# Latent attention rows: transpose and division by the row sum in one matmul with a scaled identity

## The chip, the cores and the metric

The kernel runs on one core of a Trainium2 chip. The metric is the device time of one execution in microseconds (us). The kernel before takes 1691.37 us, the median of three runs that lie between 1691.06 and 1694.24.

The core has five engines that run side by side, each taking its own instructions in order, and that wait for one another by semaphores. PE is the matrix engine: a matmul is a weight load (LDWEIGHTS, listed as PEld) followed by a MATMUL that streams the other operand through the array, and it writes into PSUM. DVE (the vector engine) and ACT (the scalar engine) do elementwise work and move results from PSUM to SBUF. POOL does a few small things, and SP issues most of the DMAs.

## The reference

Two layers of a hybrid backbone over 512 latent tokens with a prefix of 256 context tokens, width 1024, float32. Layer 0 mixes by a gated linear attention and, beside it, by a grouped attention of 8 query heads on 2 key heads of width 64; layer 1 is a gated recurrence. Each layer ends with a SwiGLU feed-forward of width 2816. The part that matters here is the attention of layer 0 for the latent rows, in which each query sees all 768 keys:

```
def _softmax_attend(q, k, v):
    s = jnp.einsum('bhgqd,bhkd->bhgqk', q, k, preferred_element_type=jnp.float32) * (ATT_HEAD_DIM ** -0.5)
    p = jax.nn.softmax(s, axis=-1).astype(v.dtype)
    return jnp.einsum('bhgqk,bhkd->bhgqd', p, v)
```

The softmax is exp(s - max) divided by the sum of its row. The second einsum sums over keys, so the kernel has to turn the probabilities: from queries on partitions to keys on partitions.

## The kernel before, in words

Tokens are handled in tiles of P = 128: LT = 4 latent tiles, NTT = 6 tiles in all, NT = 768 tokens. The attention of layer 0 is the class `Attention`. Its method `latent` (a generator, called "y" in the list of steps that sets the program's order) goes through 32 steps, 4 query tiles by 8 heads. A step i does the following, where `ahead` is 3:

- `scores` for head i: four matmuls write the 128 x 768 scores into a PSUM tile `S` (two buffers of 1024 columns). DVE takes the row extreme into `amx` (L193), ACT takes the exponential into the SBUF tile `prob` and sums each row into `asm` on the way (L195), DVE takes the reciprocal into `ars` (L196), and DVE multiplies the 768 columns of `prob` by it in place (L198).
- `turned` for head i - 3: six transposes on PE, each of a 128 x 128 block of `prob` with the identity `ident` as the other operand. The first four write one PSUM bank (tag "tr", two buffers), the last two write a bank that they share with the attention's output of the other parity (`sc0` or `sc1`). ACT copies the bank with 512 columns to `probT`; the one with 256 columns is copied by ACT, or by DVE for every fourth head (`j % 4 == 3`).
- `values` for each second head: `attO` sums the products of `probT` with the values over six key tiles, for two heads at once in the two halves of the array's columns.
- after the fourth pair of a query tile, `done` splits the output into a high and a low part (L734 on ACT, L735 on DVE) for the output projection.

Between these steps the program places others: transposes and splits of the linear attention's output (`catT`, L1288, L1289), its normalization (`gvo`), the turning of the next query tile's queries (`qT`, `qs`), a group of modulation columns (`mod_acc`), and weight splits for the next stage (`wH`, `wL`).

In this stretch all PE instructions are pinned to the order in which the code emits them; DVE and ACT are ordered by the framework's scheduler, so an edit may move their instructions. All PE instructions are issued by two helpers, so matmuls carry the line L355 (`Net.mm`) and transposes L358 (`Net.tr`), and it is the tile's name that tells them apart.

One later place of the kernel already multiplies by a scaled identity: `pair_turn` in the norm ahead of layer 1's mixer. L689 makes a tile `dg` from the identity and the inverse root mean square, and the turning of two token tiles is done in four rounds of four matmuls with it:

```
        for q in range(4):
            pt = self.tr_tile(f"hT{t}{q}").rearrange("p (k i) -> p k i", k=2)
            ...
            for kk in range(2):
                k = 2 * q + kk
                for a, (xt, dg) in enumerate(pair):
                    self.mm(pt[:, kk, a * P : (a + 1) * P], xt[:, k * P : (k + 1) * P], dg, start=True, stop=True)
```

It runs for three pairs of token tiles, so it holds 3 x 4 x 4 = 48 matmuls in the code, all of them of float32 operands with 128 columns.

Of the kernel before, what the change touches and what calls it, by code (L numbers as in the profile page):

```python
# [8 lines left out]
F32 = mybir.dt.float32  # L9
# [4 lines left out]
ALU = mybir.AluOpType  # L14
# [3 lines left out]
P = 128  # L18
# [115 lines left out]
class Attention:  # L134
# [40 lines left out]
            nc.vector.tensor_tensor(q[half[1 - n], 4 * n : 4 * n + 4, :], pv[half[n]], H.bitcast(F32), op=ALU.subtract)  # L175
        self.q[t] = q

    def scores(self, t, heads, p):

        nc, net = self.nc, self.net  # L180
        s = net.mm_tile("S")
        nk = p.shape[-1]
        w = 1024 // len(heads)
        for x, hd in enumerate(heads):
            at = w * x
            for ks in self.k[int(t >= LT)]:
                m = ks[0].shape[-1]
                for i, k in enumerate(ks):
                    net.mm(s[:, at : at + m], self.q[t][:, hd, :], k[:, hd // 4, :], start=(i == 0), stop=(i == 1))
                at += m  # L190
        sv = s.rearrange("p (x k) -> p x k", k=w)[:, :, :nk]
        mx, sm, r = (net.sm.tile([P, len(heads)], F32, tag=tag, name=tag) for tag in (("amx", "asm", "ars") if len(heads) == 1 else ("ms4", "ss4", "rs4")))
        nc.vector.tensor_reduce(mx, sv, axis=AX.X, op=ALU.min)  # L193
        for x in range(len(heads)):
            nc.scalar.activation(p[:, x, :], sv[:, x, :], AF.Exp, bias=mx[:, x : x + 1], scale=-1.0, accum_out=sm[:, x : x + 1])  # L195
        nc.vector.reciprocal(r, sm)  # L196
        for x in range(len(heads)):
            nc.vector.tensor_scalar(p[:, x, :], p[:, x, :], r[:, x : x + 1], None, op0=ALU.mult)  # L198

    def turned(self, p, pT, vector, which=None):  # L200

        nc, net = self.nc, self.net
        n = pT.shape[1]
        for b, g in enumerate(range(0, n, 4)):
            m = min(4, n - g)
            pt = net.tr_tile("pT") if b == 0 or which is None else net.sc_tile("pT", which)
            for i in range(m):
                net.tr(pt[:, i * P : (i + 1) * P], p[:, (g + i) * P : (g + i + 1) * P], net.ident)
            src = pt[:, : m * P].rearrange("p (c i) -> p c i", c=m)
            (nc.vector.tensor_copy if b in vector else nc.scalar.copy)(pT[:, g : g + m, :], src)  # L210

# [23 lines left out]
    def context(self):  # L235
# [24 lines left out]
        yield  # L260
        queries(LT + 1, "wL")
        scores(0)
        yield
        scores(1)
        yield
        turned(0)
        yield
        scores(2)
        values(0)
        yield  # L270
        scores(3)
        turned(1)
        yield
        values(1)
        yield
        self.done(LT)
        turned(2)
        yield
        values(2)
# [5 lines left out]
    def latent(self, ap):  # L285
        kl = [ap.tile([P, 2, SEQ], F32R, name=f"k{x}") for x in "HL"]
        self.k[0] = [kl] + self.k[1]
        q = lambda t: ap.tile([P, 8, P], F32R, tag="qs", bufs=2, name=f"qs{t}")
        self.keys(0, LT, kl)
        yield  # L290
        self.queries(0, q(0))
        yield

        ahead = 3
        ps, pTs, due = {}, {}, []
        for i in range(8 * LT + ahead + 2):
            t, hd = divmod(i, 8)
            if t < LT:
                ps[i] = ap.tile([P, NT], F32, tag="prob", bufs=4, name="prob")
                self.scores(t, (hd,), ps[i][:, None, :])  # L300
            j = i - ahead
            if 0 <= j < 8 * LT:
                pTs[j] = ap.tile([P, NTT, P], F32, tag="probT", bufs=4, name="probT")
                self.turned(ps.pop(j), pTs[j], (1,) if j % 4 == 3 else (), self.other())
            if due:
                t0, n, xs = due.pop()
                self.values(t0, n, xs)
                if n == 3:
                    self.done(t0)
            if 0 <= j < 8 * LT and j % 2:  # L310
                due.append((j // 8, j // 2 % 4, [pTs.pop(x) for x in (j - 1, j)]))
            if t + 1 < LT and hd == 4:
                self.queries(t + 1, q(t + 1))
            yield
# [1883 lines left out]
```

## Time and profile before

| | |
|---|---|
| time, median of three runs | 1691.37 us |
| time of the profiled execution | 1690.72 us |
| its span, first to last instruction | 1688.8 us |
| PE busy in the span | 1646.5 us (97%) |
| DVE busy | 1309.0 us (78%) |
| ACT busy | 922.0 us (55%) |
| the latent heads' turning, first to last transpose | 264.1 to 344.9 us |
| granted clock of PE, mean | 0.998 |

A row of a tile's view gives, for a group of like instructions, the line, engine, operation, output and inputs, the count, and the shortest, median and longest duration in ns. A row of the timeline gives the start and the length in us of a run of like instructions, and in brackets the time that the engine stood idle before them and what it waited for. A row of the waits says who waited for what, the sum in us, the count, and the longest. The table by stretches gives each engine's busy time and, in brackets, its instructions. Matmuls overlap each other in PE's pipeline: the sum of their durations is larger than the time that they take, and their price is read from the distance between their starts.

### The profile page before, as it was taken

How to read it: one execution, taken by the hardware profiler on the slowest of the kernel's cores; microseconds unless marked ns; L12 is line 12 of the kernel's file. 1: busy time of each engine (PE TensorE's matmuls, PEld its weight loads, DVE VectorE, ACT ScalarE, POOL GpSimd, SP SyncE). 2: the span in 40 equal slices, each digit the busy share in tenths (PEclk: the TensorE clock that was granted, in tenths of full speed). 3: DMA queues.
4: the chain of work that ended last, by engine and by line, in shares of the span. 5: the costliest groups of instructions: out<-in, count | busy, mean ns of one | idle time of the engine just before them, and what ended most of it. 6: DMA issues, size and time to landing. Idle time of an engine off the chain costs nothing.

```text
span 1688.8 us, 32537 instructions
## 1 busy us (share of the span) xinstructions
PE 1646.5 (97%) x13407; PEld 1482.6 (88%) x13407; DVE 1309.0 (78%) x2102; ACT 922.0 (55%) x1563; POOL 124.4 (7%) x129
## 2 busy tenths in 40 slices
PE   6999998999999999999999999999999999999997
PEld 5899997888999999998887888888888899999875
DVE  4889768875898988778667538788774599987977
ACT  4745567836544443445447436566564565555654
POOL 1004110011000000003102000000000100000221
PEclk9999999999999999999999999999999999999999
DMA  9651003164243444348625542121124334333793
GB/s 329 192 155 41 2 27 101 51 211 153 86 138 103 147 150 139 115 146 180 125 101 186 172 128 64 51 62 41 52 65 149 125 113 117 108 101 101 192 195 137
DMA packets 184737, 204.79 MB, mean 121 GB/s; under 512 B 7143, under 2 KB 141837, under 8 KB 184589
## 3 DMA queue, kind: packets, MB, share of 16 engines
q1 hardware_dynamic: 173632, 181.82, 34.3%
q0 software_dynamic: 9024, 17.30, 6.0%
q10 hardware_dynamic: 1932, 3.59, 0.6%
q8 instruction: 105, 1.72, 0.4%
q14 instruction: 44, 0.35, 0.1%
HBM read 193.23 MB, written 9.46 MB: 120 GB/s over the span
## 4 chain that ended last, share of the span: by engine, by line
PE 84%; DVE 7%; ACT 4%; DMA 2%; issue 2%; POOL 1%; DVEq 0%; ACTq 0%; POOLq 0%
PE nat L355 12%; PE a L355 12%; PE ff L355 8%; PE E L355 8%; PE x L355 7%; PE oproj L355 6%; PE o L355 4%; PE D L355 4%; PE b L355 4%; PE fq L355 3%; PE gqk L355 2%; PE pearly L355 2%; PE S L355 1%; PE poh L355 1%; PE attO L355 1%
## 5 line engine op out<-in xcount | busy, mean ns | idle before, releaser
L355 PE MATMUL nat<-wH,x 128*128 128x256 f32 (+2 forms) x968 | 225.4, 321 | 3.0 <-ACT x L734 2.6
L355 PEld LDWEIGHTS nat<-wH,x 128*128 128x128 f32 x968 | 162.2, 190 | 19.2 <-ACT x L734 3.6
L824 ACT CAST wH<-raw 128x1024 fp32r<-128x1024 f32 x120 | 125.0, 1050 | 95.5 <-DVE raw L849 31.8
L825 DVE TENSOR_TENSOR wL<-raw,wH 128x1024 fp32r<-128x1024 f32 x120 | 145.7, 1221 | 20.8 <-ACT wH L824 20.2
L355 PE MATMUL nat<-wL,x 128*128 128x256 f32 (+2 forms) x484 | 153.4, 317 | 0.3 <-DVE wL L770 0.3
L770 DVE TENSOR_TENSOR wL<-raw,wH 128x1024 fp32r<-128x1024 f32 (+1 forms) x83 | 98.7, 1198 | 46.1 <-ACT wH L769 45.4
L355 PE MATMUL ff<-x,wH 128*128 128x512 f32 (+1 forms) x512 | 127.6, 340 | 0.0
L668 POOL TENSOR_TENSOR rs<-ms,neghalf 128x1 f32<-128x1 f32 (+2 forms) x62 | 66.4, 1076 | 785.4 <-DVE ms L666 785.3
L769 ACT CAST wH<-raw 128x1024 fp32r<-128x1024 f32 (+1 forms) x83 | 84.9, 1035 | 69.5 <-PE ff L355 19.8
L355 PE MATMUL oproj<-wH,x 128*128 128x512 f32 x320 | 102.0, 395 | 0.4 <-ACT x L1288 0.4
L597 DVE SCALAR_TENSOR_TENSOR macc<-mraw,scT,macc 128x1024 f32<-128x1024 f32 x70 | 88.2, 1281 | 14.7 <-DMA mraw<-in_mod_w_dram 14.7
L355 PEld LDWEIGHTS nat<-wL,x 128*128 128x128 f32 x484 | 92.1, 190 | 6.0 <-DVE wL L770 0.7
L355 PEld LDWEIGHTS ff<-x,wH 128*128 128x128 f32 x512 | 87.3, 190 | 10.0
L355 PE MATMUL x<-wH,two 128*128 128x512 f32 x280 | 91.4, 396 | 0.9 <-DVE y L1796 0.7
L976 ACT COPY qkh<-arr 128x512 f32<-128x512 f32 x112 | 70.1, 642 | 36.3 <-DVE arr L981 32.2
L1721 POOL DMA_DIRECT2D t<-in_ffn_w_down_dram x36 | 41.8, 1229 | 648.2 <-DVE wL L1755 610.4
L355 PE MATMUL ff<-x,wL 128*128 128x256 f32 (+1 forms) x256 | 86.2, 337 | 0.0
L849 DVE TENSOR_TENSOR raw<-raw 128x512 f32<-128x512 f32 x120 | 82.8, 690 | 2.8
L981 DVE TENSOR_TENSOR arr<-arr,f 128x512 f32<-128x512 f32 x112 | 74.2, 687 | 1.9 <-ACT qkh L976 0.3
L355 PE MATMUL E<-x,wH 128*128 128x384 f32 (+1 forms) x320 | 70.9, 311 | 0.0
L355 PE MATMUL b<-x,wH 128*128 128x384 f32 (+1 forms) x320 | 70.6, 309 | 0.0
L355 PE MATMUL a<-T,wH 128*128 128x384 f32 (+1 forms) x320 | 70.4, 309 | 0.1
(422 smaller groups left out, 4536.8 us busy)
## 6 DMA issues: line engine op xcount, KB each, us to landing
mraw<-in_mod_w_dram SPq DMA_DIRECT2D x80, 512.0 KB, 4.6
raw<-in_ffn_w_gate_dram SPq DMA_DIRECT2D x44, 512.0 KB, 4.8
raw<-in_ffn_w_up_dram SPq DMA_DIRECT2D x44, 512.0 KB, 4.3
raw<-in_odd_w_in_dram SPq DMA_DIRECT2D x40, 512.0 KB, 3.7
t<-in_ffn_w_down_dram POOLq DMA_DIRECT2D x30, 512.0 KB, 8.0
raw<-in_ffn_w_down_dram SPq DMA_DIRECT2D x28, 512.0 KB, 7.3
mraw<-in_mod_w_dram SPq DMA_DIRECT2D x32, 256.0 KB, 6.0
raw<-in_even_w_in_dram SPq DMA_DIRECT2D x16, 512.0 KB, 4.2
```

Of the source, the lines that this page charges most:

```text
L355: return self.pin(self.nc.tensor.matmul(*a, **k))
L597: nc.vector.scalar_tensor_tensor(a, u, w, a, op0=ALU.mult, op1=ALU.add)
L668: nc.gpsimd.tensor_tensor(rs, ms, self.neghalf.to_broadcast([P, w]), op=ALU.pow)
L769: nc.scalar.copy(H[:, :m], raw[:, :m])
L770: nc.vector.tensor_tensor(L[:, :m], raw[:, :m], H[:, :m].bitcast(F32), op=ALU.subtract)
L824: self.nc.scalar.copy(H, f)
L825: self.nc.vector.tensor_tensor(L, f, H.bitcast(F32), op=ALU.subtract)
L849: add = lambda o, x, y: nc.vector.tensor_tensor(o, x, y, op=ALU.add)
L976: nc.scalar.copy(qkv[:, :, :, half, :], dst)
L981: nc.vector.tensor_tensor(dst, dst, tb, op=ALU.mult)
L1721: add = lambda o, src: self.pin(nc.gpsimd.dma_start(out=o, in_=src, accum_op=ALU.add))
```

## The change

For the latent rows the probabilities are no longer multiplied by the inverse sums. Instead DVE makes a 128 x 128 tile `dg`, the identity with its rows scaled by the inverse sums, and the six transposes of a head become six ordinary float32 matmuls of the `prob` block with `dg`: the result is the block turned, with each column scaled. There are four buffers of `dg`. Beside it, the 256-column bank is copied by DVE for every second head instead of every fourth. The context rows go on as before.

```diff
-    def scores(self, t, heads, p):
+    def scores(self, t, heads, p, dg=None):
...
         nc.vector.reciprocal(r, sm)
+        if dg is not None:
+            nc.vector.tensor_scalar(dg, net.ident, r, None, op0=ALU.mult)
+            return
         for x in range(len(heads)):
             nc.vector.tensor_scalar(p[:, x, :], p[:, x, :], r[:, x : x + 1], None, op0=ALU.mult)
...
             for i in range(m):
-                net.tr(pt[:, i * P : (i + 1) * P], p[:, (g + i) * P : (g + i + 1) * P], net.ident)
+                at, x = pt[:, i * P : (i + 1) * P], p[:, (g + i) * P : (g + i + 1) * P]
+                if dg is None:
+                    net.tr(at, x, net.ident)
+                else:
+                    net.mm(at, x, dg, start=True, stop=True)
...
-                self.scores(t, (hd,), ps[i][:, None, :])
+                dgs[i] = ap.tile([P, P], F32, tag="dg", bufs=4, name="dg")
+                self.scores(t, (hd,), ps[i][:, None, :], dgs[i])
...
-                self.turned(ps.pop(j), pTs[j], (1,) if j % 4 == 3 else (), self.other())
+                self.turned(ps.pop(j), pTs[j], (1,) if j % 2 else (), self.other(), dgs.pop(j))
```

On PE the order stays, and in the code's own count so does the number of instructions: one for one. This is what stands on PE at the third head of the first query tile (`kH`, `kL` and `kc` are the keys, high and low parts of the latent ones and those of the context, `qs` the queries), before:

```order
L358 MATMUL pT<-ident,prob 128x128 x6
L355 MATMUL attO<-probT,natk 64x128 x12
L355 MATMUL S<-kH,qs_3589 128x512
L355 MATMUL S<-kL,qs_3589 128x512
L355 MATMUL S<-kc,qs_3589 128x256 x2
```

and after (the helpers' lines have moved by eight, L355 to L363 and L358 to L366):

```order
L363 MATMUL pT<-dg,prob 128x128 x6
L363 MATMUL attO<-probT,natk 64x128 x12
L363 MATMUL S<-kH,qs_3589 128x512
L363 MATMUL S<-kL,qs_3589 128x512
L363 MATMUL S<-kc,qs_3589 128x256 x2
```

The six `pT` are now issued by the helper for matmuls; nothing has changed place. On ACT the scheduler has moved some instructions. At the start of the stage, behind the first two exponentials and the split of the context rows' output, there stood before:

```order
L734 CAST x_3653<-attO 128x4x128
L210 COPY probT<-pT 128x512
L195 ACTIVATE prob,asm<-S,amx 128x768 x2
L210 COPY probT<-pT 128x256
L210 COPY probT<-pT 128x512
L210 COPY probT<-pT 128x256
L195 ACTIVATE prob,asm<-S,amx 128x768
```

and after:

```order
L742 CAST x_3653<-attO 128x4x128
L195 ACTIVATE prob,asm<-S,amx 128x768
L217 COPY probT<-pT 128x512
L195 ACTIVATE prob,asm<-S,amx 128x768
L217 COPY probT<-pT 128x256
L217 COPY probT<-pT 128x512
L195 ACTIVATE prob,asm<-S,amx 128x768
```

The third exponential now stands ahead of the first copy, and one of the 256-column copies has gone to DVE. On DVE the copies stand between the row extremes of two heads; around the end of the first query tile (`x` here is L735, the split of that tile's output), before:

```order
L193 TENSOR_REDUCE amx<-S 128x1
L196 RECIPROCAL ars<-asm 128x1
L198 TENSOR_SCALAR prob<-prob,ars 128x768
L196 RECIPROCAL ars<-asm 128x1
L198 TENSOR_SCALAR prob<-prob,ars 128x768
L193 TENSOR_REDUCE amx<-S 128x1
L735 TENSOR_TENSOR x_3654<-attO,x_3653 128x4x128
```

and after:

```order
L193 TENSOR_REDUCE amx<-S 128x1
L196 RECIPROCAL ars<-asm 128x1
L198 TENSOR_SCALAR dg<-ident,ars 128x128
L196 RECIPROCAL ars<-asm 128x1
L198 TENSOR_SCALAR dg<-ident,ars 128x128
L743 TENSOR_TENSOR x_3654<-attO,x_3653 128x4x128
L193 TENSOR_REDUCE amx<-S 128x1
L217 COPY probT<-pT 128x256
```

Here the split of the output stands ahead of the row extreme that it stood behind, and the scaling works on 128 columns instead of 768. POOL's and SP's instructions are the same in both kernels.

More of the change, by code (lines that the diff above doesn't have):

```diff
@@ L196, in scores, with turned @@
         nc.vector.reciprocal(r, sm)
+        if dg is not None:
+            nc.vector.tensor_scalar(dg, net.ident, r, None, op0=ALU.mult)
+            return
         for x in range(len(heads)):
             nc.vector.tensor_scalar(p[:, x, :], p[:, x, :], r[:, x : x + 1], None, op0=ALU.mult)
-    def turned(self, p, pT, vector, which=None):
+    def turned(self, p, pT, vector, which=None, dg=None):
         nc, net = self.nc, self.net
@@ L294, in latent @@
         ahead = 3
-        ps, pTs, due = {}, {}, []
+        ps, pTs, dgs, due = {}, {}, {}, []
         for i in range(8 * LT + ahead + 2):
```

## The prediction, made before the changed kernel ran

> **What bounds the kernel now.** I read first the page's busy times, then a table by stretches around the place of the change, then PE's waits in that stretch.
>
> ```profile
> span 1688.8 us, 32537 instructions
> PE 1646.5 (97%) x13407; PEld 1482.6 (88%) x13407; DVE 1309.0 (78%) x2102; ACT 922.0 (55%) x1563; POOL 124.4 (7%) x129
> ```
>
> PE is nearly always busy over the whole run. That is an average, so the stage is looked at by itself: the turning of the latent heads lies between 264.1 and 344.9 us.
>
> ```profile
> 254.00:262.00 8.00, 5.20 (x49) 4.24 (x50) 6.72 (x11) 7.64 (x10) 0.61 (x1) 1.00 0.81 255
> 262.00:348.00 86.00, 81.16 (x819) 68.08 (x816) 70.44 (x131) 67.23 (x142) 1.28 (x1) 1.00 0.20 69
> 348.00:1689.00 1341.00, 1322.55 (x9321) 1195.00 (x9319) 1038.10 (x1538) 704.57 (x1115) 83.47 (x81) 1.00 0.43 123
> ```
>
> The columns are the stretch, its length, and busy time with instruction count of PE, PEld, DVE, ACT and POOL, then granted clock, DMA share, GB/s. In the 86.0 us from 262 on, PE is busy 81.16, DVE 70.44, ACT 67.23, at full clock. PE stands still for 4.8 us, and the waits on PE in this stretch account for all of it:
>
> ```profile
> PE pT L358 <- DVE x L735: 1.8, 2, 1.3
> PE S L355 <- ACT prob L195: 1.8, 2, 1.4
> PE pT L358 <- DVE probT L210: 0.5, 2, 0.3
> PE qT L358 <- ACT probT L210: 0.5, 1, 0.5
> PE catT L358 <- DVE qs L175: 0.2, 1, 0.2
> ```
>
> 1.8 + 1.8 + 0.5 + 0.5 + 0.2 = 4.8 us. So here PE sets the pace, and whatever DVE or ACT save can be worth 4.8 us at most, while work added to PE has no more than 4.8 us of idle time to go into. None of these waits is on L198, the scaling that the change removes.
>
> **The six products of a head on PE.** The diff puts one matmul for one transpose, so the question is what each holds PE for. The rows by tile, of the turning and of the later place that already multiplies by a scaled identity of the same type and size:
>
> ```profile
> L358 PE MATMUL pT<-ident,prob x224: 270/272/330, 234.7 to 344.9; 128*128 128x128 f32 x112
> L355 PE MATMUL hT<-dg,xr x96: 270/275/377, 906.9 to 946.7; 128*128 128x128 f32 x96
> ```
>
> Two things are to be seen. The durations, 272 and 275 ns, are alike and say nothing of the price, since PE overlaps its instructions. The counts do: the code has 48 matmuls with `dg` at the later place (three pairs, four rounds, four each) and the trace has 96, so a float32 matmul is run as two weight loads and two MATMULs. Of the transposes the code has 192 in the latent rows and 32 in the context rows, and the trace has 224: one each. What one record takes is read from the timeline, from a run of each kind:
>
> ```profile
> 277.08 0.82 PE L358 MATMUL pT<-ident,prob 128*128 128x128 f32 x6
> 277.65 0.47 PE L355 MATMUL S<-kH,qs 128*128 128x512 f32 x1
> ...
> 906.90 1.05 PE L355 MATMUL hT<-dg,xr 128*128 128x128 f32 x8
> 907.70 0.48 PE L355 MATMUL x<-wH,aH 128*128 128x512 f32 x1
> ```
>
> Six transposes span 0.82 us; less the last one's own 0.272, five distances make 0.548, or 0.110 us each. Eight records with `dg` span 1.05; less 0.275, seven distances make 0.775, or 0.111 us each. The pace of a record is the same, only there are two per matmul. A head goes from 6 x 0.110 = 0.66 us to 12 x 0.111 = 1.33 us, 0.67 more, and 32 heads give **+21.5 us** of PE. This is my firmest term; from the same two runs, timed from the start to the start of the next tile, it is 6 x 0.095 = 0.57 against 12 x 0.100 = 1.20, or +20.2 us, which I take as its low end. The high end is 32 x (12 x 0.112 - 6 x 0.108) = +22.3, from the rounding of the rows.
>
> The Trainium skill's page "TensorE: Matmul & The Clock Gate", Part 4, gives a PE transpose as about 275 ns in one kernel's context and says that the fast clock does not engage for it. By that price a transpose would be dearer than the two records, and 192 x (0.222 - 0.275) = -10 us. The trace agrees with the 275 as a duration (272 here), and disagrees with it as a price: the transposes start 0.110 us apart, and the granted clock of the stretch is 1.00.
>
> **DVE.** The rows of what goes and of the nearest thing to what comes:
>
> ```profile
> L198 DVE TENSOR_SCALAR prob<-prob,ars x32: 600/620/624, 261.7 to 341.4; 128x768 f32<-128x768 f32 x32
> L689 DVE TENSOR_SCALAR dg<-ident,rs x6: 281/285/287, 896.5 to 934.7; 128x128 f32<-128x128 f32 x6
> L210 DVE COPY probT<-pT 128x256 f32<-128x256 f32 x8 | 3.3, 414 | 3.2 <-PE pT L358 3.2
> L210 ACT COPY probT<-pT 128x256 f32<-128x256 f32 x24 | 9.2, 382 | 0.5 <-PE pT L358 0.3
> ```
>
> 32 x (0.620 - 0.285) = 10.7 us less, and eight copies more (32 of 256 columns in all, 16 instead of 8 on DVE), 8 x 0.414 = 3.3: DVE loses 7.4 us of its 70.4. **ACT** loses 8 x 0.382 = 3.1 of its 67.2. Both I cost at nothing by themselves: PE is busy beside them, and they can only shorten PE's 4.8 us of waits. The way from the sum of a row to the first product is shorter by 0.335 us for each head; three heads of lead hide that already, as no wait of `pT` on `ars` or L198 shows. A `dg` buffer is used again by the fourth head after it, whose scores PE makes only behind the products that read it, so no wait comes from there.
>
> **What becomes of PE's 4.8 us.** PE now arrives later at each wait, by up to 0.67 us a head, unless what it waits for follows from PE itself. The four largest:
>
> ```profile
> 266.39 0.47 PE L355 MATMUL S<-kH,qs 128*128 128x512 f32 x1 [1.44 <-ACT prob L195]
> 288.59 0.41 PE L358 MATMUL pT<-ident,prob 128*128 128x128 f32 x2 [1.30 <-DVE x L735]
> 312.70 0.66 PE L358 MATMUL qT<-ident,natq 128*128 128x128 f32 x4 [0.51 <-ACT probT L210]
> 332.01 0.44 PE L358 MATMUL pT<-ident,prob 128*128 128x128 f32 x2 [0.50 <-DVE x L735]
> ```
>
> The first is the backlog of exponentials on ACT at the stage's start. One head's turning lies ahead of it (0.67), and the third exponential now stands ahead of a 512-column copy, whose median is 577 ns by this row:
>
> ```profile
> L210 ACT COPY probT<-pT x60: 371/577/613, 235.3 to 345.1; 128x512 f32<-128x512 f32 x36, 128x256 f32<-128x256 f32 x24
> ```
>
> Together 1.25, so about 0.2 of 1.44 stays. The waits on L735 follow from PE: the bank is that of the attention's output, which ends on PE a few matmuls earlier and must pass ACT and DVE. Between that end and the waiting product PE has four products of the first bank, 4 x (0.222 - 0.110) = 0.45 us more work, so 1.30 becomes 0.85 and 0.50 becomes 0.05. The order of DVE puts L735 ahead of a row extreme there, which may take away more, and I leave that out. The remaining waits, 4.8 - 1.44 - 1.80 = 1.6 us, I take as gone, as PE is late by several heads' worth and DVE and ACT have less to do. That leaves 0.2 + 0.85 + 0.05 = 1.1 us, so 3.7 us of the added work falls into idle time.
>
> A new wait could come from DVE's copies, 16 instead of 8, each behind whatever DVE is doing. Two of the eight of before held PE, for 0.5 us together. Eight more at that rate give 0.5, at 0.3 each 2.4. With 0.67 us more between two uses of the bank I take nothing.
>
> **After the stage.** The output projection and the feed-forward follow at once:
>
> ```profile
> 347.00:380.00 33.00, 33.00 (x155) 27.29 (x152) 25.46 (x27) 10.75 (x15) 4.43 (x4) 1.00 0.68 222
> sum 193.00, PE 193.00 PEld 178.31 DVE 153.51 ACT 94.96 POOL 11.30; mean PE 38.60 PEld 35.66 DVE 30.70 ACT 18.99 POOL 2.26
> ```
>
> From 347 to 540 us PE is busy 193.0 of 193.0, so what the stage loses is handed on whole. Farther on there is 1341.00 - 1322.55 = 18.5 us in which PE is not busy; a lead that DVE and the DMAs win while PE is late can give little back there, as it would have to last through 190 us without a gap.
>
> **The sum.** +21.5 - 3.7 = +17.8 us on the profiled execution's 1690.72 gives 1708.5. The median of the runs stands 0.65 above that execution, so 1691.37 + 17.8 = 1709.2: I say **1709**. Its own range is 1705 (20.2 of PE, all 4.8 absorbed, another 1.5 given back later) to 1713 (22.3 of PE, 1 absorbed).
>
> **The rivals.**
>
> - *Faster: ACT and DVE set the pace, and PE has room.* It speaks for it that the chain of work that ended last passes through DVE and ACT repeatedly in this stage, L198 among them (start, length, piece):
>
> ```profile
> 270.95 0.62 DVE prob L198
> ...
> 304.55 0.59 DVE prob L198
> ```
>
> If all the added products fitted into idle time and all five waits went, it would be 1691.4 - 4.8 = 1686.6. It decides from the point at which PE has 21 us of idle time in the stage, and it has 4.8. Chance 0.03.
> - *The matmul with `dg` is one record, as the transpose.* Then the change does what its words say, division for nothing, and DVE's 7.4 us can only shorten waits: 1687 to 1691, middle 1689. Against it stand 96 records for 48 matmuls. Chance 0.03.
> - *Transposes hold PE for their listed duration.* -10 us, 1681; the pace of 0.110 us speaks against it, chance 0.01. This is the skill's price above.
> - *No cushion.* The waits stay, and DVE's copies add theirs: 21.5 + 2.4 = +23.9, 1715. For it: waits that hang on PE's own work move along with it. Against it: DVE and ACT each have less to do. From 1713 up, chance 0.12.
> - *More given back.* DVE's and the DMAs' lead shortens later waits: 1700 to 1705. Against it: no gap for 190 us. Chance 0.07.
>
> **How the numbers follow.** The forecast has 0.74 (1705 to 1713). To leave out no more than 2 in 10 I take in most of the no-cushion and half of the given-back case: 1703 to 1715. No change means within 0.2%, 3.4 us, which is about what a measurement of this kernel can tell. Faster by more than that: 0.03 + 0.01 and a third of the one-record case, 0.05; the same: 0.02; slower: 0.93.
>
> **What the profile after would show.** `pT` with `dg` counted 384 times, in runs of twelve at 0.111 us, and only 32 transposes left under the old form; if there are 192, the main term is wrong. The scaling at 285 ns instead of 620, and DVE's busy time in the stage some 7 us lower. PE's waits in the stage near 1 us instead of 4.8, the wait of `S` on the exponential nearly gone, a rest on L735's successor. PE busy without a gap behind the stage, each landmark there some 18 us later. A wait of `pT` on DVE's copies above 1 us would speak for no cushion.

## The result: 15 us slower

The changed kernel takes 1706.92 us (median of four runs, 1706.46 to 1708.3) against 1691.64 for the kernel before on the same chip, a ratio of 1.0088 with a 95% interval from 1.0076 to 1.0099, so 12.9 to 16.8 us. Timed again it was 1705.49 against 1691.71, ratio 1.0078 (1.0066 to 1.0091). The profiled execution took 1706.46, 15.7 more than the one of before.

The page after, and the stretch in which the latent heads are turned, now 102 us long instead of 86 (columns as before):

```profile
span 1704.7 us, 32915 instructions
PE 1666.8 (98%) x13599; PEld 1507.0 (88%) x13599; DVE 1303.2 (76%) x2110; ACT 921.8 (54%) x1555; POOL 124.0 (7%) x129
```

```profile
262.00:364.00 102.00, 101.49 (x1005) 91.65 (x1006) 65.77 (x141) 65.98 (x134) 1.00 (x1) 0.98 0.18 60
```

PE has 192 instructions more (13599 against 13407) and is now busy for 101.49 of 102 us. DVE was busy for 70.4 us in the 86 before and for 65.8 in the 102 after, and the run is slower all the same.

The products and the making of `dg`, in the view by tile:

```profile
L363 PE MATMUL pT<-dg,prob x384: 272/275/421, 266.1 to 361.9; 128*128 128x128 f32 x192
L366 PE MATMUL pT<-ident,prob x32: 270/272/328, 235.4 to 259.3; 128*128 128x128 f32 x32
L198 DVE TENSOR_SCALAR dg<-ident,ars x32: 274/286/290, 262.5 to 356.5; 128x128 f32<-128x128 f32 x32
```

Two records per product, 384 for 192, and the median duration of one hardly differs from that of a transpose. What a head costs PE is seen in the timeline, first of the kernel after, then of the kernel before, each with a run that is followed by the next scores and one that is followed by the output's products:

```profile
280.67 1.50 PE L363 MATMUL pT<-dg,prob 128*128 128x128 f32 x12
281.93 0.47 PE L363 MATMUL S<-kH,qs 128*128 128x512 f32 x1
...
282.70 1.50 PE L363 MATMUL pT<-dg,prob 128*128 128x128 f32 x12
284.13 1.53 PE L363 MATMUL attO<-probT,natk 128*64 128x128 f32 x24
```

```profile
274.06 0.82 PE L358 MATMUL pT<-ident,prob 128*128 128x128 f32 x6
274.81 1.53 PE L355 MATMUL attO<-probT,natk 128*64 128x128 f32 x24
```

From start to start it is 1.26 and 1.43 us after. Before it was 0.57 (the pair at 277.08 and 277.65 that the prediction shows) and 0.75. That is 0.68 to 0.69 us a head, or 21.9 us for 32 heads. The waits on PE in the stage, after:

```profile
PE attO L363 <- ACT probT L217: 2.1, 1, 2.1
PE pT L366 <- DVE kL L162: 0.6, 1, 0.6
PE pT L363 <- DVE probT L217: 0.2, 1, 0.2
```

The first two lie ahead of the first latent product and were there before (2.1 and 0.6). Of the 4.8 us behind it, 0.2 is left.

How the 15.7 us of the profiled pair come about: the stage, from the first latent scores to the last products of the output, takes 16.2 us more. The first pair of rows is of before, the second of after:

```profile
255.83 0.47 PE L355 MATMUL S<-kH,qs 128*128 128x512 f32 x1
...
345.95 1.52 PE L355 MATMUL attO<-probT,natk 128*64 128x128 f32 x22
```

```profile
256.56 0.48 PE L363 MATMUL S<-kH,qs 128*128 128x512 f32 x1
...
362.89 1.52 PE L363 MATMUL attO<-probT,natk 128*64 128x128 f32 x22
```

That is 106.33 - 90.12 = 16.2. It is +21.9 for the products; -5.7 for stalls that are gone; +1.2 because in this execution PE ran for 3.4 us at half clock just there, so that the eight scores matmuls ahead of the first product took 2.72 us (263.36 to 266.08) instead of 1.50; and -0.8 because three matmuls of the output projection, which stood among the last heads' transposes, are now behind them. (The description of the change says that PE's order stays. This is the exception to it.) These terms sum to 16.6, 0.4 more than measured. Behind the stage the 0.8 comes back, and the execution of before had its own stretch at half clock at 902 us, which the one after has not: about 1.7 us. So 16.2 + 0.7 of later start + 0.8 - 1.7 = 16.0, against 15.9 between the spans. That the two stretches at half clock nearly cancel in this pair is chance.

The stalls need a word, since they are larger than the list of waits says. In the kernel before I took, for each run of six transposes, the distance from its start to the start of the next tile, less the shortest such distance with the same neighbour. Ten runs are longer, by 1.69, 1.49, 0.72, 0.67, 0.57, 0.50, 0.49, 0.43, 0.06 and 0.06 us: 6.7 us in all, where the list has 4.8. After, four runs are longer, by 1.0 together, and 0.36 of that is no wait but the first run's share of the half-clock stretch. Two examples from the timeline of before:

```profile
286.69 0.60 PE L358 MATMUL pT<-ident,prob 128*128 128x128 f32 x4
288.59 0.41 PE L358 MATMUL pT<-ident,prob 128*128 128x128 f32 x2 [1.30 <-DVE x L735]
288.84 0.60 PE L358 MATMUL qT<-ident,natq 128*128 128x128 f32 x4
...
306.01 0.82 PE L358 MATMUL pT<-ident,prob 128*128 128x128 f32 x6
307.15 0.50 PE L355 MATMUL S<-kH,qs 128*128 128x512 f32 x1 [0.32 <-ACT prob L195]
```

The first run takes 288.84 - 286.69 = 2.15 us where an unstalled one takes 0.66, a stall of 1.49 that is listed as 1.30. The second takes 1.14 instead of 0.57, a stall of 0.57 that is listed as 0.32. The duration of the last record before a wait still counts as busy while nothing new can start.

### The profile page after: what moved, and what is told of

Its sections match the earlier page's. It is cut to its first block, busy times and chain, and to the rows that moved or that the text cites. A ratio compares the mean times of both kernels' runs of the same rounds, so it can differ in the third digit from the quotient of the medians.

```text
span 1704.7 us, 32915 instructions
## 1 busy us (share of the span) xinstructions
PE 1666.8 (98%) x13599; PEld 1507.0 (88%) x13599; DVE 1303.2 (76%) x2110; ACT 921.8 (54%) x1555; POOL 124.0 (7%) x129
## 4 chain that ended last, share of the span: by engine, by line
PE 86%; DVE 6%; ACT 3%; DMA 2%; issue 2%; POOL 1%; ACTq 0%; POOLq 0%; DVEq 0%
PE nat L363 11%; PE a L363 11%; PE ff L363 8%; PE E L363 7%; PE x L363 7%; PE oproj L363 5%; PE o L363 5%; PE b L363 4%; PE D L363 4%; PE fq L363 3%; PE pT L363 2%; PE gqk L363 2%; PE pearly L363 2%; PE S L363 2%; PE q L363 2%
## 5 line engine op out<-in xcount | busy, mean ns | idle before, releaser
L363 PE MATMUL nat<-wH,x 128*128 128x256 f32 (+2 forms) x968 | 225.4, 321 | 3.0 <-ACT x L742 2.6
L363 PEld LDWEIGHTS nat<-wH,x 128*128 128x128 f32 x968 | 162.2, 190 | 19.2 <-ACT x L742 3.7
L363 PE MATMUL nat<-wL,x 128*128 128x256 f32 (+2 forms) x484 | 153.4, 317 | 0.3 <-DVE wL L778 0.3
L363 PE MATMUL ff<-x,wH 128*128 128x512 f32 (+1 forms) x512 | 127.6, 340 | 0.0
L363 PE MATMUL oproj<-wH,x 128*128 128x512 f32 x320 | 101.9, 395 | 0.6 <-ACT x L1296 0.6
L363 PEld LDWEIGHTS nat<-wL,x 128*128 128x128 f32 x484 | 92.1, 190 | 6.0 <-DVE wL L778 0.8
L363 PEld LDWEIGHTS ff<-x,wH 128*128 128x128 f32 x512 | 87.3, 190 | 10.0
L363 PE MATMUL x<-wH,two 128*128 128x512 f32 x280 | 90.5, 392 | 0.9 <-DVE y L1804 0.7
L363 PE MATMUL ff<-x,wL 128*128 128x256 f32 (+1 forms) x256 | 86.2, 337 | 0.0
L363 PE MATMUL E<-x,wH 128*128 128x384 f32 (+1 forms) x320 | 70.9, 311 | 0.0
L363 PEld LDWEIGHTS oproj<-wH,x 128*128 128x128 f32 x320 | 59.5, 188 | 12.8 <-ACT x L1296 1.1
L363 PE MATMUL a<-x,dH 128*128 128x384 f32 (+1 forms) x320 | 70.3, 309 | 0.3 <-ACT early L905 0.3
```

The lines of the kernel that those rows point to most:

```text
L363: return self.pin(self.nc.tensor.matmul(*a, **k))
```

## The experiments

Theory A was that the loss is the 192 second records, less the stalls that PE's added work fills by itself. The main rivals were that the savings on DVE and ACT soften the loss (B), that a float32 product is dearer in itself (D), and that the copies on DVE matter (F).

**The products alone.** The kernel before, with this edit in `turned` for the latent rows:

```diff
-                net.tr(at, x, net.ident)
+                net.mm(at, x, net.ident, start=True, stop=True)
```

> Only the products: the latent rows' transposes become float32 matmuls with the plain identity, while DVE's scaling of 768 columns and the copies stay as before. Theory A (PE sets the pace; 192 more records cost 21.9 us of PE, less the time that PE stood still before, which it fills by itself): 14 to 17 us slower than before, 1706 to 1709, about as the changed kernel. Theory B (what softened the loss from 21.5 to 15.3 us is the 7.4 us that DVE and the 3.1 us that ACT saved): without these savings the waits stay, 19 to 22 us slower, 1711 to 1714.

Measured: 1704.72 us against 1691.23, ratio 1.0086 (1.0072 to 1.0100), 13.5 us slower. No saving on DVE or ACT, and yet it is not slower than the changed kernel. Its waits on PE in the stage:

```profile
PE attO L359 <- ACT probT L214: 2.1, 1, 2.1
PE pT L362 <- DVE kL L162: 0.6, 1, 0.6
PE S L359 <- ACT prob L195: 0.4, 1, 0.4
```

The waits are gone just as well with the large scaling still on DVE. So what took them away is PE's own slowness, not the work spared elsewhere. B falls. The loss is half a microsecond less than A's lowest; the first measurement of the changed kernel stood 2.2 us above it, which is followed up below.

**Everything but the products.** The changed kernel, with plain transposes in place of the products (so it leaves out the division by the row sums):

```diff
-                    net.mm(at, x, dg, start=True, stop=True)
+                    net.tr(at, x, net.ident)
```

> Everything but the products: the small scaled identity is made and the scaling of 768 columns is gone, the copies are divided as in the changed kernel, but the blocks are turned by plain transposes (the scaled identity is not used, so the division by the sums is left out). PE's work is that of before, so only waits on PE can go. Theory A1 (the time that PE stands still in the stage is about 7 us, counted from start to start of its instructions): 4 to 7 us faster, 1684.5 to 1687.5. Theory A2 (it is the 4.8 us of the list of waits): 2 to 4.8 us faster, not below 1686.8. Theory C (DVE and ACT have nothing to do with the pace): within 1.5 us of before.

Measured: 1691.28 us against 1691.23, ratio 1.0002 (0.9993 to 1.0011). That can't be told from none. I had expected 2 to 7 us, since DVE has less to do:

```profile
262.00:348.00 86.00, 81.47 (x821) 68.36 (x819) 63.32 (x139) 65.29 (x134) 1.01 (x1) 1.00 0.20 69
```

DVE is busy for 63.3 us instead of 70.4, and PE for as long as before. The waits on PE in it, without the two ahead of the stage:

```profile
PE pT L363 <- DVE x L740: 1.5, 2, 1.3
PE S L360 <- ACT prob L195: 1.4, 1, 1.4
PE pT L363 <- DVE probT L214: 1.2, 4, 0.5
PE qT L363 <- DVE x L1294: 0.2, 1, 0.2
```

4.3 us of 4.8 are still there. The two largest single waits, 1.3 and 1.4 us, hang on a chain that starts on PE (the output's last products, ACT's cast, DVE's subtraction, then the bank is free) and on ACT's exponential. The waits for copies even went from 0.5 to 1.2. Both A1 and A2, which I held, fall, and C's range holds: the part of the change that was to gain is, as a whole, worth nothing here.

**The copies alone.** The kernel before with `(1,) if j % 2 else ()` instead of `(1,) if j % 4 == 3 else ()`.

> The kernel before with one edit: DVE instead of ACT copies the 256-column bank for every second head, not every fourth. The vector part as a whole measured no difference (1691.3 against 1691.2). Theory F (it is the sum of two: the smaller scaling gains, the copies on DVE lose about as much): 2 to 5 us slower than before, 1693 to 1696. Theory C (neither matters, since PE waits for work that hangs on PE itself): within 1.5 us of before.

Measured: a ratio of 1.0005 (0.9996 to 1.0013), 1693.14 against 1691.51 in the medians. The interval ends at 2.2 us, at the low edge of F, so the times do not decide between F and C. The trace leans to F. PE's waits for copies on DVE are 2.1 us in the stage, where there were 0.5:

```profile
PE pT L358 <- DVE probT L210: 2.1, 5, 0.8
```

From start to start this kernel's stalls are 9.1 us where the kernel before has 6.7. A half-clock stretch makes 0.4 of that, so about 2 us are new. The kernel with everything but the products has the same copies and the small scaling, and its stalls are 6.7 us again. So in these traces, of one execution each, the vector part is a loss of about 2 us by the copies and a gain of about 2 us by the smaller scaling. In the times neither is clear of the noise, and the smaller scaling with the old copies was not run.

**The transposes twice.** The kernel before, each latent transpose issued two times into the same place:

```diff
-                net.tr(at, x, net.ident)
+                for _ in range(2):
+                    net.tr(at, x, net.ident)
```

> The kernel before with each transpose of the latent rows issued twice into the same place: 192 more records, all of them transposes; scaling and copies as before. Theory A (a record holds PE for 0.109 us whatever its kind, and the loss is 192 records): 13 to 16 us slower, 1704.5 to 1707.5, within 2 us of the kernel with the products alone. Rival D (a float32 product is dearer in itself, by its longer weight load of 0.19 against 0.14 us or by changing from one kind to the other): 8 to 12 us slower, well below the products alone.

Measured: 1705.18 us, ratio 1.0087 (1.0073 to 1.0101), 14.0 us slower, the same as the products alone within 0.5 us. A run of six doubled transposes, from the timeline:

```profile
280.44 1.47 PE L359 MATMUL pT<-ident,prob 128*128 128x128 f32 x12
281.66 0.47 PE L356 MATMUL S<-kH,qs 128*128 128x512 f32 x1
```

1.22 us for twelve, against 1.26 for the twelve records of six products. The kind of record hardly matters; their number does. D falls for float32 products.

**One record a product.** The changed kernel with `prob` and `dg` allocated as F32R, the type that the projections' operands have.

> The changed kernel with the probabilities and the scaled identity in the shortened float type that the projections use, so that the product is taken in one pass of lower precision; all else as changed. Theory A (the loss is the second record of each product): PT has 192 records with the scaled identity at 0.11 us, PE's work is that of before, and the time is that of the kernel with the vector part alone, 1684.5 to 1688. Rival D (a product with a scaled identity costs more than a transpose even as one record): 1692 to 1700. Rival E (it is two records here too): as changed, 1705 to 1708.

Measured: 1695.50 us against 1691.23, ratio 1.0027 (1.0018 to 1.0037). The trace has 192 records for the 192 products, as expected:

```profile
L363 PE MATMUL pT<-dg,prob x192: 221/274/476, 265.6 to 348.0; 128*128 128x128 f32 x192
```

Halving the records takes away about 10 us of the loss, the bulk of it, but 4.3 us remain where A expected none. Its list of waits has 2.5 us of `pT` on DVE's copies, so the next run took these copies back.

**One record, old copies.** The same with `j % 4 == 3`.

> The one-record product (probabilities and scaled identity in the shortened float type), with the copies divided as in the kernel before (DVE every fourth head). Theory F (what was left of the one-record kernel's loss, 1695.5 against 1691.2, is waits for copies on DVE): 1688 to 1692, so at least 3 us below the one-record kernel. Theory J (the loss is in the product's form): within 1.5 us of it, 1694 to 1697.

Measured: 1695.17 us, ratio 1.0025 (1.0015 to 1.0035). F falls, the copies are not it. J's range fits, but the trace of the first one-record kernel doesn't bear out its reason, that the product's form is dearer on PE:

```profile
277.54 0.78 PE L363 MATMUL pT<-dg,prob 128*128 128x128 f32 x6
278.16 0.45 PE L363 MATMUL S<-kH,qs 128*128 128x512 f32 x1
...
278.92 0.78 PE L363 MATMUL pT<-dg,prob 128*128 128x128 f32 x6
279.63 1.53 PE L363 MATMUL attO<-probT,natk 128*64 128x128 f32 x24
```

From start to start six products take 0.62 and 0.71 us, where six transposes take 0.57 and 0.75. What differs is the clock. The profiles of both one-record kernels have two stretches at half clock within the stage (at 262.6 and 344.6 us in the first, at 263.1 and 310.8 in the second), where every other kernel has one or none. In the first one the stage, from the first latent scores to the last products of the output, takes 93.0 us against 90.1, though three matmuls of the output projection (0.8 us) have moved out of it here too. Two stretches of up to 1.7 us each are most of that. Over all 11 executions the mean granted clock is 0.9951 and 0.9958, against 0.9970 and 0.9966 for the kernel before on the same chips. A stretch lowers a run's mean by 0.001, so by this estimate there are about two and one more per run, 3.2 us of the 4.3 and 1.4 us of the 3.7. Why there are more of them was not tried, and the rest of the loss stays open.

**Half the heads.** The changed kernel with `dg` for the first two query tiles only; the other 16 heads are scaled and transposed as before:

```diff
-                dgs[i] = ap.tile([P, P], F32, tag="dg", bufs=4, name="dg")
+                dgs[i] = ap.tile([P, P], F32, tag="dg", bufs=4, name="dg") if t < 2 else None
```

> The change for the first 16 of the 32 heads (two query tiles); the other heads' probabilities are scaled on DVE and transposed as before, copies as in the changed kernel. By distances from start to start the products add 0.685 us a head, 11.0 us; before, PE stood still behind transposes for 4.2 us in the first 16 heads and 2.5 us in the others. Theory G (each stall is filled where PE is slower, and stays where it is not): 11.0 - 4 = 7 us slower, 1697.5 to 1699.5. Theory H (being late is enough, so the other half's stalls go too): 4 to 5.5 us slower, 1695 to 1697. Theory I (cost goes by records, no cushion): 10 to 11.5 us slower, 1701 to 1703.

Measured: 1699.77 us against 1691.51, ratio 1.0043 (1.0029 to 1.0058), 8.3 us slower; G's range ends at 1699.5, and the interval, 4.9 to 9.8 us, reaches into H's. The profile decides between G and H. In the changed half two runs are stalled, by 0.7 and 0.4 us, where before there were 4.2; in the unchanged half the runs are stalled by 0.68, 0.46, 0.72, 0.50 and 0.06, 2.4 us, where before there were 2.5. A row of that half, which stood with 0.50 at 332.01 before:

```profile
PE pT L366 <- DVE x L743: 0.5, 1, 0.5
```

So a stall is filled where PE itself does more between the event and the need, and being 8 us late does not help.

**The old copies in the changed kernel, and the two again side by side.** The changed kernel with `j % 4 == 3`, and then the changed kernel and the products alone on one chip.

> The changed kernel with the copies divided as in the kernel before (DVE every fourth head). Theory A (PE has so much to do that no copy holds it): within 1.2 us of the changed kernel, 1705.5 to 1708. Theory F (the copies on DVE cost here too, and explain why the products alone measured 2.2 us below the changed kernel): 1704 to 1705.3.

> The changed kernel itself, timed with more rounds on the same chip as the products alone. Theory A (the loss is the records less the stalls that they fill; the savings on DVE and ACT are worth nothing): the two kernels within 1.2 us of each other, both 14 to 15.5 us slower than before. Theory F (the DVE copies of the changed kernel hold PE): 1.5 to 3 us slower than the products alone. Theory B (the savings count): faster than the products alone by 3 us or more.

> The products alone, beside the changed kernel on one chip. Theory A: 1705 to 1707, within 1.2 us of the changed kernel. Theory F: 1.5 to 3 us below it. Theory B: 3 us or more above it.

Measured: 1705.61 us with the old copies, ratio 1.0081 (1.0068 to 1.0094): in A's range, but the interval covers F's too. Side by side the changed kernel took 1705.49 (1.0078, 1.0066 to 1.0091) and the products alone 1706.28 (1.0084, 1.0070 to 1.0098). They differ by 0.8 us in the other direction than the 2.2 of the first measurement, which was scatter. Neither F's nor B's difference is there, and A holds: with or without the savings on DVE and ACT, the products cost 14 to 15 us (13.5 to 15.3 in the measurements).

## Why the prediction was right, and which term was mis-sized

The forecast was 1709, in 1703 to 1715, and 1706.92 was measured: +15.3 instead of +17.8. The main reason, the second record of each product, was the right one. What PE's idle time takes off was put too small, and one reason given for it was wrong.

- *The six products of a head.* Right: 384 records, 0.111 us apart ((1.50 - 0.275) / 11 in the rows above), 21.9 us against the 21.5 forecast. The low end of 20.2, taken from starts to starts in the two old runs, was an error. In a run's time from its start to the next tile's start, the last step is shorter than the others: 0.80 us for eight records is 7 x 0.111 and 0.02. Scaling it by 12/8 takes that short step one and a half times instead of once. With four full steps more it is 0.80 + 4 x 0.111 = 1.24 against 0.57, or 21.6 us for 32 heads.
- *DVE and ACT cost and gain nothing by themselves.* Right as a sum: the vector part as a whole changed the time by nothing that can be measured. By the traces it is two effects of about 2 us that cancel, neither of which is in the sum. `dg` took 286 ns against 285. DVE's sum over the span fell by 5.8 us (1309.0 to 1303.2) instead of 7.4; ACT's hardly moved (922.0 to 921.8) where I had 3.1 less; what made up for its eight copies was not traced.
- *What becomes of PE's 4.8 us.* This is the step that was mis-sized: 3.7 us of absorbed work were forecast, and 5.7 were measured (6.1 without the 0.36 that half clock adds to a run). It failed in its first number. The 4.8 us of the list leave out the part of each wait that lies under the preceding record's duration; from start to start the stalls were 6.7 us. Then I let 1.1 us stay, and 0.2 stayed in the list, 1.0 by starts. In particular the two waits on L735 went altogether, where 0.9 was to stay. These are DVE's rows at the two places before:

```profile
286.89 0.95 DVE L193 TENSOR_REDUCE amx<-S 128x1 f32<-128x768 f32 x1
287.76 0.68 DVE L735 TENSOR_TENSOR x<-attO,x 128x512 fp32r<-128x512 f32 x1
...
331.27 0.68 DVE L735 TENSOR_TENSOR x<-attO,x 128x512 fp32r<-128x512 f32 x1
331.87 0.95 DVE L193 TENSOR_REDUCE amx<-S 128x1 f32<-128x768 f32 x1
```

At the first place the subtraction stood behind a row extreme, and after it stands ahead of one; I had seen this order and left it out. The kernel with everything but the products has it behind, and the wait of 1.3. At the second place it stood ahead of the row extreme before, too, so the order is not the cause there: it ended 1.04 us behind the start of PE's run before and 0.61 after, and the four products' 0.45 us more do the rest. For the remaining 1.6 us I had given as a reason that PE is late by several heads' worth. Half the heads shows this to be wrong: behind 16 slowed heads, 2.4 of 2.5 us of stalls stayed.

- *DVE's new copies.* Taken as nothing, and in the changed kernel nothing it was: 0.2 us of waits after. Without the products they make 2.1 us of waits (the copies alone).
- *After the stage.* Right: what was lost was handed on. From the output's last products to the end it took 1341.8 us against 1342.8, and this 1 us is three moved matmuls (+0.8) and the stretch at half clock of before (-1.7). So nothing speaks for "more given back".
- *The rivals.* "No cushion" falls by the stalls that went. "One record" falls by the count. "Faster" was the other side of the claim that PE sets the pace, and the vector part alone, with no measurable gain, shows it wrong also in the form that I had thought possible, a few microseconds of waits. The price of a transpose by its listed duration falls by the doubled transposes, which cost 192 x 0.109 us less the stalls, not 192 x 0.272.

## What to carry to other kernels

Before an elementwise pass is folded into a matmul, count the records that the matmul makes, and price them by the distance between their starts: a transpose and a float32 product with the identity have the same listed duration here, and one holds PE twice as long. On the engine that sets the pace the idle time, too, is to be read from start to start, since the list of waits gave 4.8 us where 6.7 were to be had. And work spared on an engine that others wait for need not show in the time: here the vector part took 7 us of work off DVE and gained nothing, since some of the waits were chains that begin on the waiting engine itself, and, by the traces, since the copies moved to DVE cost what the smaller scaling won.

## What the runs showed of the hardware that was not expected

PE falls to half clock for 3.4 us at a time, and at different places in different executions. The stretches of before (at 902 us, behind waits of 1.57 and 0.37 us) and of after (at 263 us, behind the wait of 2.09 us), in the table by stretches:

```profile
902.30:905.50 3.20, 3.20 (x9) 2.42 (x9) 2.68 (x5) 1.15 (x2) 1.37 (x2) 0.50 0.82 254
```

```profile
263.40:266.50 3.10, 3.10 (x13) 2.71 (x11) 2.12 (x4) 1.06 (x2) 0.00 (x0) 0.50 0.93 329
```

The wait at 260 us, 2.1 us long, is in all twelve profiled kernels. In seven of them a half-clock stretch follows it, in five it does not, the kernel before among these. The traces show what sets them apart. Within each trace the clock's changes lie whole multiples of 3.413 us apart, so they fall on a grid. In the seven the wait lies inside one step of this grid: after, it lasts from 260.25 to 262.34 us, in the step from 260.00 to 263.41, where the stretch begins. In the five a step ends within the wait: before, the stretch at 902.21 less 188 steps gives a step's end at 260.51, and the wait lasts from 259.51 to 261.60. So at this place it is the execution's place on the grid that decides. At the shorter waits around 900 us a stretch follows in some executions and not in others, and in the one-record kernels two follow waits of no more than 0.8 and 1.2 us each; no rule for these is shown.

Each stretch can cost up to 1.7 us, half its length. In the first set of experiments the 21 executions of the kernel before lie between 1688.2 and 1694.6, and the longer ones have the lower mean clock: eight at 0.998 take 1690.4 us on average, two at 0.995 take 1694.2. Differences of 2 us between two profiles need a look at the clock first.

The other thing is the one-record product, which keeps a loss of 4 us over a transpose of the same count and pace. More stretches at half clock go with it; their cause, and the rest of the loss, stay open.
